# Head pairs in an attention, longer runs of expert weights, and expert pairs with few tokens laid out twice

## The chip, the cores and the metric

One core of one Trainium2 chip runs the whole program. The metric is the device time of one launch in microseconds (us).

The engines are named as the profile does: PE is TensorE's matmul, PEld its weight load, DVE is VectorE, ACT ScalarE, POOL GpSimd, SP SyncE, which here only issues DMAs. The kernel before took 2064.22 us, the median of three runs (2059.43 to 2067.44).

## The reference

A chain of two blocks on 256 tokens of width 1024, in float32. The first block has gated feed-forwards and two mixers; its first mixer (`combine_a`, `latent_attention`) is an attention of 8 query heads of width 64 over 512 keys (256 of the sequence, 256 of a context) beside a pooling branch. The second block has two layers; each has a mixer and then a mixture of experts:

```python
def grouped_moe(h, router_w, router_b, w_gate, w_up, w_down):
    t = h.reshape(B_ * S, D)
    scores = jax.nn.sigmoid((t @ router_w).astype(jnp.float32))
    ...
    top_w = top_s / jnp.sum(top_s, axis=-1, keepdims=True)
    combine = jnp.einsum('nk,nke->ne', top_w, jax.nn.one_hot(top_idx, N_EXPERTS, dtype=jnp.float32))
    for e in range(N_EXPERTS):
        he = jax.nn.silu(t @ w_gate[e]) * (t @ w_up[e])
        y = y + combine[:, e:e + 1] * (he @ w_down[e]).astype(jnp.float32)
```

There are 16 experts of width 512; each token goes to two of them. Gate and up are 1024 x 512, down is 512 x 1024, so an expert has 6 MB of weights in float32 and a layer 100.7 MB.

## The kernel before

**Layout.** The activations are held feature by token (`XT`, 128 x 8 x 256). Dense products in the earlier stages split both operands into a high and a low part and issue three products each (`mm3`, lines 448 to 450).

**Order of the work.** The kernel is written in Python on a framework that places the instructions of each engine in an order of its own, by priority and by when their inputs are there, and sets all semaphores; where `keep_in_program_order` or `pin` stands, the order of the text is kept. In the attention, `pipeline(units, width, bg, rate)` steps up to `width` units (Python generators) in turn, each from one `yield` to the next, and after each round takes `rate` steps of the background work `bg` (here dense products and the output projection).

**Attention of the first mixer** (`attend`, lines 1073 to 1107). A unit is one head for one block of 128 tokens: 16 units, 5 in flight. `t` is one of four pairs of heads, `tt` the token block, `s` which head of the pair; a head's features lie on partitions 0 to 63 or 64 to 127. A unit has four steps: the scores, one 128 x 512 product over 64 features (line 1079); the softmax on VectorE and ScalarE (lines 1082 to 1088); four transposes (line 864) and their copies; the product with the values (line 1100), four products that write 64 partitions of the tile `po`.

**The experts** (`moe`, from line 1578). Experts p and p + 8 make pair p; eight pairs run one after the other. A pair has 128 slots. The planner (lines 1739 to 1764, small VectorE operations after the router) counts the tokens of each expert and gives the two experts 64 and 64 slots, or 96 and 32 where one has over 64 tokens and the other at most 32; tokens that don't fit go to extra rounds at the end. `onehot` (line 1770) makes the 0/1 matrix that says which token sits in which slot; `gather` (line 1810) multiplies the normalised tokens `n_` by it and adds the modulation's shift `s`.

`pair` (line 1863) then runs gate and up (`products`, line 1841), each over eight blocks of 128 rows of K, for each block one product for each segment of slots. Its arms, chosen at run time by a register `gr_` that PE reads, are

```python
SEG = {2: ((0, 64, 0), (64, 64, 1)),
       3: ((0, 32, 0), (32, 32, 0), (64, 32, 0), (96, 32, 1)),
       1: ((0, 32, 0), (32, 32, 1), (64, 32, 1), (96, 32, 1))}
```

as (first slot, slots, expert). Each segment is a group of columns of the array with the slots as the stationary side and 512 weight columns moving; a float32 product is two instructions in the trace. After gate and up come SiLU (ScalarE) times up (VectorE), four transposes (line 1875) and a copy, the two halves of `down`, and `back`, which spreads the result over the tokens (line 1895). `nxt` places the next pair's gather between these steps.

**The weights of the experts.** `pieces` and `piece` issue them on SP's queue. A piece is 1 MB: half of K for gate and up, half of the columns for down, of one expert; 12 for a pair in the order gate, up, down, 96 for a layer. They go round a ring of 20 buffers; the DMA for piece n waits until PE has read piece n - 20. From piece 20 on, two pieces are loaded together in halves of 512 KB. Row k * 128 + p of the weights goes to partition p, so each partition gets 512 columns, 2 KB, from each of four rows.

Of the kernel before, what the change touches and what calls it, by code (L numbers as in the profile page):

```python
# [7 lines left out]
F32 = mybir.dt.float32  # L8
# [3 lines left out]
OP = mybir.AluOpType  # L12
# [5 lines left out]
KD = 8  # L18
# [107 lines left out]
def build(tc, I, out, dump=None, upto=99):  # L126
    nc = tc.nc
    coff, ctot = _const_layout()
    with ExitStack() as ctx:
# [831 lines left out]
        with ExitStack() as c1:  # L961
# [112 lines left out]
            def attend(t, tt, s):  # L1074

                hs = slice(s * 64, (s + 1) * 64)
                need(("A", t), "Ak", "Av")
                p = psum("sc")
                mm(p, qr[t][hs, tt * 128:(tt + 1) * 128], kr[hs, :], start=True, stop=True)
                yield  # L1080
                st = wk.tile([128, 4], F32, name="st", tag="st", bufs=8)
                V.reduce_max(st[:, 0:1], p, axis=AX.X)
                r = qs[:, t * 4 + tt * 2 + s:t * 4 + tt * 2 + s + 1]
                V.tensor_scalar(st[:, 1:2], st[:, 0:1], r, -1.0, op0=OP.mult, op1=OP.mult)
                x = tmp("e")
                S.activation(x, p, AF.Exp, bias=st[:, 1:2], scale=r, accum_out=st[:, 2:3])
                V.reciprocal(st[:, 3:4], st[:, 2:3])
                V.tensor_scalar(x, x, st[:, 3:4], None, op0=OP.mult)
                yield
                i0 = (t * 4 + tt * 2 + s) % 4 * 512  # L1090
                PT = pts[0][:, i0:i0 + 512].rearrange("p (a b) -> p a b", a=4)
                for _, pt in transposes([x[:, i * 128:(i + 1) * 128] for i in range(4)]):
                    V.tensor_copy(PT[:, 0:2], four(pt)[:, 0:2])
                    S.activation(PT[:, 2:4], four(pt)[:, 2:4], AF.Copy)
                yield
                if (tt, s) == (0, 0):
# [5 lines left out]
                if (tt, s) == (1, 1):  # L1102
# [34 lines left out]
            pipeline([attend(t, tt, s) for t in range(4) for tt in range(2) for s in range(2)], 5,  # L1137
                     [ch, part(op, 1), drain(), until(*[("Ao", t) for t in range(3)]), part(op, 2)], 0.8)
# [440 lines left out]
        def moe(l, a, op, pre=None, post=None):  # L1579


            with ExitStack() as c1:
# [3 lines left out]

                bufs = [hp.tile([128, KD * W], F32, name="ew", tag=t)[:, :2048] for t in ("hh", "hl")]
# [11 lines left out]
                def pieces(upto):  # L1599
                    while len(wpiece) < min(upto, len(todo)):  # L1600
# [3 lines left out]
                        for ks in (slice(0, 2), slice(2, 4)) if again else (slice(0, 4),):  # L1604
# [3 lines left out]
                def piece(buf, w, nm, hf, ks=slice(0, 4)):  # L1608
                    if nm == "exp_w_down_2":
                        w = w[:, hf * 512:(hf + 1) * 512]  # L1610
                    else:
                        w = w[hf * 512:(hf + 1) * 512]
                    w = w.rearrange("(k p) c -> p k c", p=128)
                    if isinstance(buf, list):
                        for k in range(ks.start, ks.stop):
                            nc.sync.dma_start(buf[k], w[:, k])
                    else:
                        nc.sync.dma_start(buf.rearrange("p (k c) -> p k c", k=4)[:, ks], w[:, ks])
# [5 lines left out]
                pieces(8)  # L1624

# [110 lines left out]

                A2 = [128, 2, 8]
# [10 lines left out]
                V.tensor_scalar(ga[:, 1], ga[:, 0], -1.0, 128.0, op0=OP.mult, op1=OP.add)  # L1748
                gi = mp.tile([128, 8], I32, name="gi")
                V.tensor_scalar(gi, ga[:, 0], 0.03125, None, op0=OP.mult)  # L1750
# [302 lines left out]
```

## Time and profile before

| | |
|---|---|
| time, three runs | 2064.22 us median (2059.43 to 2067.44) |
| the profiled execution | 2066.13 us, span 2064.4 us |
| PE busy | 1961.0 us, 95% of the span |
| VectorE, ScalarE busy | 1289.3 us (62%), 734.3 us (36%) |
| mean granted TensorE clock | 0.977 |
| DMA | 534.77 MB, 259 GB/s on average |
| attention of the first mixer | about 491 to 563 us |
| first expert stage, first gate product to last product | about 1413 to 1648 us |
| second expert stage | about 1819 to 2056 us |

A stage is found by its lines in the timeline of PE. "Busy" counts an engine's instructions from their start to a modelled end; products overlap, so the time that a product really takes is the distance of its start from the next one's. A wait is put down to what ended last before the instruction started; "issue" is time in which the engine waited for nothing that the profile shows. [...] A DMA's share can be above 1.00, as packets overlap.

### The profile page before, as it was taken

How to read it: one execution, taken by the hardware profiler on the slowest of the kernel's cores; microseconds unless marked ns; L12 is line 12 of the kernel's file. 1: busy time of each engine (PE TensorE's matmuls, PEld its weight loads, DVE VectorE, ACT ScalarE, POOL GpSimd, SP SyncE). 2: the span in 40 equal slices, each digit the busy share in tenths (PEclk: the TensorE clock that was granted, in tenths of full speed). 3: DMA queues.
4: the chain of work that ended last, by engine and by line, in shares of the span. 5: the costliest groups of instructions: out<-in, count | busy, mean ns of one | idle time of the engine just before them, and what ended most of it. 6: DMA issues, size and time to landing. Idle time of an engine off the chain costs nothing. (4 is left out here: it accounts for less than half of the span.)

```text
span 2064.4 us, 34691 instructions
## 1 busy us (share of the span) xinstructions
PE 1961.0 (95%) x14344; PEld 1605.7 (78%) x14344; DVE 1289.3 (62%) x2188; ACT 734.3 (36%) x1075; POOL 67.9 (3%) x60
## 2 busy tenths in 40 slices
PE   6999999999999999999999999997999799889998
PEld 5889899887699999999999999974444388744443
DVE  6357677758697979787797867853222387433222
ACT  3322222244354455445654445441000167500001
POOL 0000000011010010001010010000000010000000
PEclk8999999999999999999999999998999999889999
DMA  8678797734196959776496946479999654889995
GB/s 292 242 252 295 246 328 268 263 85 123 62 331 224 318 194 330 257 259 212 163 324 214 319 145 195 144 286 333 386 385 382 233 165 154 307 306 386 384 382 189
DMA packets 307696, 534.77 MB, mean 259 GB/s; under 512 B 12717, under 2 KB 167713, under 8 KB 294177
## 3 DMA queue, kind: packets, MB, share of 16 engines
q1 hardware_dynamic: 306960, 531.55, 73.5%
q8 instruction: 162, 2.65, 0.5%
q14 instruction: 46, 0.37, 0.1%
q10 hardware_dynamic: 528, 0.20, 0.0%
HBM read 530.64 MB, written 1.06 MB: 258 GB/s over the span
## 5 line engine op out<-in xcount | busy, mean ns | idle before, releaser
L448 PE MATMUL pa<-hh,whl 128*128 128x258 f32 (+1 forms) x880 | 252.3, 287 | 4.2 <-ACT hh L516 4.2
L449 PE MATMUL pa<-hl,whl 128*128 128x258 f32 (+1 forms) x880 | 249.3, 283 | 2.9 <-DVE hl L517 2.9
L448 PE MATMUL pb<-hh,whl 128*128 128x258 f32 (+1 forms) x880 | 249.1, 283 | 0.8 <-ACT s L564 0.8
L450 PE MATMUL pa<-hh,whl 128*128 128x258 f32 (+1 forms) x880 | 249.0, 283 | 0.0
L449 PE MATMUL pb<-hl,whl 128*128 128x258 f32 (+1 forms) x880 | 248.6, 282 | 0.0
L450 PE MATMUL pb<-hh,whl 128*128 128x258 f32 (+1 forms) x880 | 248.5, 282 | 0.0
L418 ACT ACTIVATE whl<-w13r 128x2048 fp32r<-128x2048 f32 x88 | 168.6, 1916 | 189.4 <-PE pb L450 93.6
L324 DVE SCALAR_TENSOR_TENSOR macc<-modw,cst,macc 128x1024 f32<-128x1024 f32 (+1 forms) x182 | 220.0, 1236 | 14.2 <-DMA modw<-in_w_mod_dram 13.5
L419 DVE TENSOR_TENSOR whl<-w13r,whl 128x2048 fp32r<-128x2048 f32 x88 | 201.7, 2292 | 39.8 <-ACT whl L418 39.8
L450 PE MATMUL py<-gh,whl 128*128 128x256 f32 (+1 forms) x704 | 216.8, 308 | 2.1 <-DVE whl L419 2.1
L448 PE MATMUL py<-gh,whl 128*128 128x256 f32 (+1 forms) x704 | 218.3, 310 | 0.1
L449 PE MATMUL py<-gl,whl 128*128 128x256 f32 (+1 forms) x704 | 216.3, 307 | 0.0
L448 PE MATMUL lin<-hh,whl 128*128 128x258 f32 x640 | 188.5, 295 | 5.7 <-DMA c_below<-in_consts_dram 5.0
L449 PE MATMUL lin<-hl,whl 128*128 128x258 f32 x640 | 182.2, 286 | 3.0 <-DVE hl L517 3.0
L450 PE MATMUL lin<-hh,whl 128*128 128x258 f32 x640 | 181.7, 284 | 0.0
L448 PEld LDWEIGHTS pa<-hh,whl 128*128 128x128 f32 x880 | 166.4, 189 | 12.2 <-ACT hh L516 4.4
L449 PEld LDWEIGHTS pa<-hl,whl 128*128 128x128 f32 x880 | 167.5, 190 | 3.5 <-DVE hl L517 3.3
L448 PEld LDWEIGHTS pb<-hh,whl 128*128 128x128 f32 x880 | 166.6, 189 | 1.8 <-ACT s L564 1.0
L450 PEld LDWEIGHTS pa<-hh,whl 128*128 128x128 f32 x880 | 167.1, 190 | 0.4 <-issue 0.4
L450 PEld LDWEIGHTS pb<-hh,whl 128*128 128x128 f32 x880 | 166.5, 189 | 0.4 <-issue 0.4
L449 PEld LDWEIGHTS pb<-hl,whl 128*128 128x128 f32 x880 | 166.7, 189 | 0.0
L418 ACT ACTIVATE whl<-w2r 128x768 fp32r<-128x768 f32 (+3 forms) x80 | 90.7, 1143 | 161.0 <-PE py L450 95.7
(444 smaller groups left out, 3796.6 us busy)
## 6 DMA issues: line engine op xcount, KB each, us to landing
w13r<-in_ffn_w_dram SPq DMA_DIRECT2D x86, 1024.0 KB
modw<-in_w_mod_dram SPq DMA_DIRECT2D x62, 1024.0 KB
ew<-in_exp_w_down_dram SPq DMA_DIRECT2D x108, 512.0 KB
modw<-in_ada_w_dram SPq DMA_DIRECT2D x48, 1024.0 KB
ew<-in_exp_w_gate_dram SPq DMA_DIRECT2D x92, 512.0 KB
ew<-in_exp_w_up_dram SPq DMA_DIRECT2D x92, 512.0 KB
w2r<-in_ffn_w_dram SPq DMA_DIRECT2D x18, 1536.0 KB
ew<-in_exp_w_gate_dram SPq DMA_DIRECT2D x16, 1024.0 KB
```

What stands on the lines that cost most here:

```text
L324: V.scalar_tensor_tensor(acc[h], x, c, acc[h], op0=OP.mult, op1=OP.add)
L418: S.activation(h, src, AF.Copy)
L419: V.tensor_sub(l, src, h.bitcast(F32))
L448: mm(p, ah, bh, start=start, stop=False)
L449: mm(p, ah, bl, start=False, stop=False)
L450: mm(p, al, bh, start=False, stop=stop)
```

## The change

**Attention.** A unit is now a pair of heads: `attend(t, tt)`, 8 units, 3 in flight, 1.1 background steps for each round in place of 0.8. The two score products stand next to each other, and the value products of the two heads alternate.

```diff
-                p = psum("sc")
-                mm(p, qr[t][hs, tt * 128:(tt + 1) * 128], kr[hs, :], start=True, stop=True)
+                ps, xs, pt_ = [psum("sc") for _ in range(2)], [], []
+                for s, p in enumerate(ps):
+                    hs = slice(s * 64, (s + 1) * 64)
+                    mm(p, qr[t][hs, tt * 128:(tt + 1) * 128], kr[hs, :], start=True, stop=True)
...
                 for i in range(4):
-                    mm(po[hs, tt * 128:(tt + 1) * 128], vn[:, i, s * 64:(s + 1) * 64], PT[:, i], start=i == 0,
-                       stop=i == 3, skip_group_check=True)
+                    for s in range(2):
+                        mm(po[s * 64:(s + 1) * 64, tt * 128:(tt + 1) * 128], vn[:, i, s * 64:(s + 1) * 64], pt_[s][:, i],
+                           start=i == 0, stop=i == 3, skip_group_check=True)
...
-            pipeline([attend(t, tt, s) for t in range(4) for tt in range(2) for s in range(2)], 5,
-                     [ch, part(op, 1), drain(), until(*[("Ao", t) for t in range(3)]), part(op, 2)], 0.8)
+            pipeline([attend(t, tt) for t in range(4) for tt in range(2)], 3,
+                     [ch, part(op, 1), drain(), until(*[("Ao", t) for t in range(3)]), part(op, 2)], 1.1)
```

**Runs of 8 KB.** Partition p now gets neighbouring rows of the weights: for gate and up rows 8p to 8p + 7, in two pieces of four rows; for down rows 4p to 4p + 3, in two pieces of two full rows. A piece is one run of 8 KB for each partition. A piece of down now holds half of K and all columns. Pieces are loaded in halves only from piece 84 on.

```diff
-                        for ks in (slice(0, 2), slice(2, 4)) if again else (slice(0, 4),):
+                        for ks in (slice(0, 2), slice(2, 4)) if n >= 84 else (slice(0, 4),):
...
-                    if nm == "exp_w_down_2":
-                        w = w[:, hf * 512:(hf + 1) * 512]
-                    else:
-                        w = w[hf * 512:(hf + 1) * 512]
-                    w = w.rearrange("(k p) c -> p k c", p=128)
+                    w = w.rearrange("(p h k) c -> h p (k c)", p=128, h=2)[hf]
...
-                        nc.sync.dma_start(buf.rearrange("p (k c) -> p k c", k=4)[:, ks], w[:, ks])
+                        cs = slice(ks.start * 512, ks.stop * 512)
+                        nc.sync.dma_start(buf[:, cs], w[:, cs])
...
-                            products(pd, hT, 4, lambda k: (w_("exp_w_down_2", dd), k), gr_, ks)
+                            products(pd, hT, 4, lambda k: (w_("exp_w_down_2", k // 2), k % 2 * 2 + dd), gr_, ks)
```

The features have to be permuted to match: the normalised tokens are written so when they leave PSUM, and the shift `s` takes the same order by a DMA to DRAM and one back, on ScalarE's queue.

```diff
+                by_p = dr.tile([8, 128], F32, name=f"by_p{l}")
+                nc.scalar.dma_start(by_p.rearrange("k p -> p k"), s)
+                sP = mp.tile([128, KD], F32, name="sP")
+                nc.scalar.dma_start(sP, by_p.rearrange("a b -> (a b)").rearrange("(p k) -> p k", k=KD))
...
-                        S.activation(n_[:, tt, i * 512:(i + 1) * 512], pT[tt, i], AF.Copy, scale=rst[:, tt:tt + 1])
+                        S.activation(n_[:, tt].rearrange("t (k p) -> t k p", k=KD)[:, :, i * 64:(i + 1) * 64],
+                                     pT[tt, i].rearrange("t (p k) -> t k p", k=KD), AF.Copy, scale=rst[:, tt:tt + 1])
```

**Light pairs.** Where both experts of a pair have at most 32 tokens, the planner gives them slots 0 to 31 and 32 to 63, and `onehot` sets the same tokens again in slots 64 to 127. A fourth arm runs four column groups: the first copy over the first half of K, the second over the other half.

```diff
+                light = mp.tile([128, 8], F32, name="light")
+                V.tensor_mul(light, c32[:, 0], c32[:, 1])
+                l64 = mp.tile([128, 8], F32, name="l64")
+                V.tensor_scalar(l64, light, 64.0, None, op0=OP.mult)
...
+                V.tensor_add(gf[:, 0], l64, ga[:, 0])
+                V.tensor_scalar(gi, gf[:, 0], 0.03125, None, op0=OP.mult)
+
+                V.scalar_tensor_tensor(gf[:, 1], light, -32.0, ga[:, 0], op0=OP.mult, op1=OP.add)
...
+                    def arm_light():
+                        h = n_k // 2
+                        for k in range(h) if ks is None else range(ks[0] // 2, ks[-1] // 2 + 1):
+                            for o in range(4):
+                                ws, kp = w_(k + o // 2 * h)
+                                mm(p[o * 32:o * 32 + 32, :], x[:, k + o // 2 * h, o * 32:o * 32 + 32], ws[o % 2][kp],
+                                   start=k == 0, stop=k == h - 1, skip_group_check=True)
...
                         with tc.If(gr_ == 2) as c:
                             arm(2)
                         with c.Else():
-                            with tc.If(gr_ == 3) as c2:
-                                arm(3)
-                            with c2.Else():
-                                arm(1)
+                            with tc.If(gr_ == 4) as c1_:
+                                arm_light()
+                            with c1_.Else():
+                                with tc.If(gr_ == 3) as c2:
+                                    arm(3)
+                                with c2.Else():
+                                    arm(1)
```

The copies are added when gate and up are turned: in every pair, each of the two results is copied out of PSUM, and four products with a 128 x 128 matrix take the place of the four transposes. `summing` makes that matrix with one VectorE operation: the identity, with a second diagonal 64 apart in a light pair. SiLU and the multiplication follow on the turned results. The stationary side of these products is read with a step of four floats.

```diff
+                    def turned(raw):
+                        p = psum("tr")
+                        for i in range(4):
+                            pin(mm(p[:, i * 128:(i + 1) * 128], raw.rearrange("s (j k) -> s k j", k=4)[:, i], sm_,
+                                   start=True, stop=True))
+                        return p
                     products(pg, xg_b, KD, lambda k: (w_("exp_w_gate_2", k // 4), k % 4), gr_)
+                    graw, uraw = tm(), tm()
+                    S.activation(graw, pg, AF.Copy)
                     products(pu, xg_b, KD, lambda k: (w_("exp_w_up_2", k // 4), k % 4), gr_)
-                    act = tm()
-                    S.activation(act, pg, AF.Silu)
-                    V.tensor_mul(act, act, pu)
+                    tg = turned(graw)
+                    V.tensor_copy(uraw, pu)
                     sw, ohT = pl
+                    hT_ = tm()
+                    S.activation(hT_, tg, AF.Silu)
                     nxt(0)
-                    hT = four(tm())
-                    p = psum("tr")
-                    for i in range(4):
-                        pin(PE.transpose(p[:, i * 128:(i + 1) * 128], act[:, i * 128:(i + 1) * 128], ident))
-                    V.tensor_copy(hT, four(p))
+                    tu = turned(uraw)
+                    V.tensor_mul(hT_, hT_, tu)
+                    hT = four(hT_)
                     nxt(1)
```

## Rows read from the trace of the kernel before

**Rows 1.** Windows, core 0, three stretches; columns: us, busy (x instructions) per engine, clock, DMA, GB/s

```profile
491.00:563.00 72.00, 68.11 (x386) 45.89 (x385) 49.97 (x132) 30.60 (x71) 0.00 (x0) 0.95 0.15 46
1413.00:1648.00 235.00, 223.26 (x1195) 105.61 (x1194) 63.41 (x134) 18.57 (x28) 0.00 (x0) 0.99 0.96 351
1819.00:2056.00 237.00, 225.98 (x1588) 104.67 (x1587) 62.14 (x132) 16.76 (x26) 0.00 (x0) 0.99 0.93 341
```

**Rows 2.** Waits of PE, 1412:1648; columns: us in total, times, longest us

```profile
PE ga L1817 <- issue: 5.9, 3, 2.3
PE pu L1848 <- issue: 2.0, 1, 2.0
```

**Rows 3.** Waits of PE, 1818:2064

```profile
PE pu L1848 <- issue: 2.6, 1, 2.6
PE pu L1848 <- DMA ew<-in_exp_w_down_dram: 2.1, 1, 2.1
```

**Rows 4.** Timeline of SP's DMA issues, 1735:2050; columns: start us, us, engine line op

```profile
1802.11 4.66 SPq L1616 DMA_DIRECT2D ew<-in_exp_w_up_dram  x4
1823.68 5.48 SPq L1618 DMA_DIRECT2D ew<-in_exp_w_down_dram  x8
```

**Rows 5.** Timeline of PE, pair 4 of the second expert stage, 1937:1966

```profile
1937.43 7.09 PE L1848 MATMUL pg<-ew,nx 128*64 128x512 f32 x32
1944.35 7.04 PE L1848 MATMUL pu<-ew,nx 128*64 128x512 f32 x32
1951.32 2.05 PE L1817 MATMUL ga<-oh,nx 128*128 128x128 f32 x16
1953.21 0.60 PE L1875 MATMUL tr<-c_ident,tm 128*128 128x128 f32 x4
1953.64 1.95 PE L1817 MATMUL ga<-oh,nx 128*128 128x128 f32 x16
1955.52 7.09 PE L1848 MATMUL pd<-ew,tm 128*64 128x512 f32 x32
1962.54 1.22 PE L1895 MATMUL py<-dd 128*128 128x256 f32 x8
...
1965.30 7.09 PE L1848 MATMUL pg<-ew,nx 128*64 128x512 f32 x32
```

**Rows 6.** DMA view, 1820:2040; columns: queue, packets, MB, share of 16 engines

```profile
q1 hardware_dynamic: 41440, 79.70, 98.5%
q8 instruction: 32, 0.52, 1.0%
```

**Rows 7.** Timeline of PE, pair 1 of the second expert stage, 1848:1863

```profile
1848.19 7.07 PE L1848 MATMUL pg<-ew,nx 128*32 128x512 f32 x64 [0.95 <-PE py L1895]
1855.09 7.05 PE L1848 MATMUL pu<-ew,nx 128*32 128x512 f32 x64
```

**Rows 8.** DMA view, 1841:2036

```profile
DMA packets 38442, 74.34 MB, mean 381 GB/s; under 512 B 2353, under 2 KB 2353, under 8 KB 38411
```

**Rows 9.** DMA view, 566:570

```profile
DMA packets 224, 1.70 MB, mean 426 GB/s; under 512 B 16, under 2 KB 16, under 8 KB 16
```

**Rows 10.** Timeline of VectorE, 1809:1813

```profile
1811.87 0.42 DVE L1773 TENSOR_TENSOR oh<-c_iota,slot 128x256 f32<-128x256 f32 x1
```

**Rows 11.** Timeline of PE, attention of the first mixer, 488:566

```profile
491.63 1.13 PE L1079 MATMUL sc<-kr,qr 64*128 64x512 f32 x4
...
497.24 1.12 PE L1079 MATMUL sc<-kr,qr 64*128 64x512 f32 x2
...
501.36 1.09 PE L1100 MATMUL po<-pts,vn 128*64 128x128 f32 x8
```

**Rows 12.** Windows, core 0, two stretches of the same attention

```profile
510.00:520.00 10.00, 9.19 (x55) 6.26 (x54) 9.49 (x27) 5.49 (x13) 0.00 (x0) 1.00 0.39 124
520.00:530.00 10.00, 8.23 (x30) 4.82 (x30) 6.18 (x16) 3.84 (x10) 0.00 (x0) 0.66 0.27 86
```

**Rows 13.** Page, part 5: the costliest groups

```profile
L448 PEld LDWEIGHTS pa<-hh,whl 128*128 128x128 f32 x880 | 166.4, 189 | 12.2 <-ACT hh L516 4.4
```

More of the change, by code (lines that the diff above doesn't have):

```diff
@@ L1080, in attend @@
                 yield
[L1081 to L1088, printed above, removed]
@@ L1089, in attend @@
-                yield
[L1090 to L1094, printed above, removed]
+                for s, p in enumerate(ps):
+                    st = wk.tile([128, 4], F32, name="st", tag="st", bufs=8)
+                    V.reduce_max(st[:, 0:1], p, axis=AX.X)
+                    r = qs[:, t * 4 + tt * 2 + s:t * 4 + tt * 2 + s + 1]
+                    V.tensor_scalar(st[:, 1:2], st[:, 0:1], r, -1.0, op0=OP.mult, op1=OP.mult)
+                    x = tmp("e")
+                    S.activation(x, p, AF.Exp, bias=st[:, 1:2], scale=r, accum_out=st[:, 2:3])
+                    V.reciprocal(st[:, 3:4], st[:, 2:3])
+                    V.tensor_scalar(x, x, st[:, 3:4], None, op0=OP.mult)
+                    xs.append(x)
@@ L1095, in attend @@
+                yield
+                for s, x in enumerate(xs):
+                    i0 = (tt * 2 + s) * 512
+                    PT = pts[0][:, i0:i0 + 512].rearrange("p (a b) -> p a b", a=4)
+                    for _, pt in transposes([x[:, i * 128:(i + 1) * 128] for i in range(4)]):
+                        V.tensor_copy(PT[:, 0:2], four(pt)[:, 0:2])
+                        S.activation(PT[:, 2:4], four(pt)[:, 2:4], AF.Copy)
+                    pt_.append(PT)
                 yield
-                if (tt, s) == (0, 0):
+                if tt == 0:
@@ L1772, in onehot @@
                     oh = mp.tile([128, 2, 128], F32, name="oh", tag="oh")
-                    V.tensor_tensor(oh, iota1[:, None, :].to_broadcast([128, 2, 128]),
-                                    slot[:, :, p:p + 1].to_broadcast([128, 2, 128]), op=OP.is_equal)
+                    V.tensor_tensor(oh[:, :, 0:64], iota1[:, None, 0:64].to_broadcast([128, 2, 64]),
+                                    slot[:, :, p:p + 1].to_broadcast([128, 2, 64]), op=OP.is_equal)
+                    V.scalar_tensor_tensor(oh[:, :, 64:128], iota1[:, None, 64:128].to_broadcast([128, 2, 64]),
+                                           l64[:, p:p + 1], slot[:, :, p:p + 1].to_broadcast([128, 2, 64]),
+                                           op0=OP.subtract, op1=OP.is_equal)
                     return oh
@@ new lines, in summing, with pair @@
+                def summing(p):
+                    x = (w0, w1)[p % 2]
+                    i2 = ident.rearrange("p (h j) -> p h j", h=2)
+                    V.scalar_tensor_tensor(x.rearrange("p (h j) -> p h j", h=2), i2[:, ::-1, :], light[:, p:p + 1], i2,
+                                           op0=OP.mult, op1=OP.add)
+                    return x
+                def pair(pl, w_, gr_, sm_, nxt=lambda i: None, last_=False):
+                    pg, pu = psum("pg"), psum("pu")
+                    def turned(raw):
[4 more added lines that the diff above has]
+                        return p
@@ L1919, in reg @@
                 def reg(p):
-                    return nc.values_load(gi[0:1, p:p + 1], engines=[ENG.PE], min_val=1, max_val=3)
+                    return nc.values_load(gi[0:1, p:p + 1], engines=[ENG.PE], min_val=1, max_val=4)
                 regs = {0: reg(0)}
@@ L1941, in moe @@
                         ohs[p + 1] = onehot(p + 1)
-                    pair(pl[p], lambda nm, hf: [wpiece[p, e, nm, hf] for e in range(2)], regs[p], nxt, p == 7)
+                    pair(pl[p], lambda nm, hf: [wpiece[p, e, nm, hf] for e in range(2)], regs[p], summing(p), nxt, p == 7)
                     pieces(12 * p + 12 + RING)
@@ L2000, in w_ @@
                         return got[nm, hf]
-                    pair(places(oh2, w2_, 0), w_, None, last_=True)
+                    pair(places(oh2, w2_, 0), w_, None, ident, last_=True)
         op = even(mods["a0"])
```

14 lines of the change are left out of this document (6 added, 8 removed).

## The prediction

> **What bounds the kernel now.** I read the page first, then the stretches, the waits and the timeline of the three stages that the change touches, then the DMA view.
>
> The page calls PE 95% busy over the whole span, which says little by itself, because stages with different limits are averaged. By stretch [rows 1], PE is busy 68.1 of 72 us in the attention of the first mixer, 223.3 of 235 in the first expert stage and 226.0 of 237 in the second. DMA runs at 0.15, 0.96 and 0.93 of its capacity there. So in both expert stages two resources look full at once, and the waits have to say which one PE is held by. In the first expert stage PE's two largest waits are "issue", 5.9 and 2.0 us, in which it waits for no data, and no wait on weights is listed [rows 2]. In the second there is one wait on weights, 2.1 us [rows 3]. PE is therefore the bound of both, with DMA just behind it. The reason DMA can hide at all is the ring of 20 weight pieces, which is full when a stage begins: the last pieces are issued at 1802.11, the next ones at 1823.68, when the first pair has used some up [rows 4].
>
> One expert pair on PE is read off the start times [rows 5]: gate 6.92 us, up 6.97, gather 1.89, transposes 0.43, gather 1.88, down 7.02, the rest 2.76 to the next gate; 27.87 in all, 223 for eight. The 76 pieces that are not in the ring at the start are 79.7 MB, which is what the SP queue moved from 1820 to 2040 [rows 6].
>
> **The expert pairs, part by part.** The trace doesn't show how many tokens an expert has. The reference's routing, worked out on its inputs, gives for the eight pairs of the first layer 52/29, 24/50, 16/20, 50/55, 9/48, 29/33, 26/18, 32/21, and of the second 12/79, 12/81, 28/72, 22/78, 21/17, 25/8, 20/14, 14/9. The four pairs with 72 to 81 tokens are those that run in 32-slot segments (x64 in place of x32) [rows 5, 7], so trace and counts agree. Both counts at most 32: pairs 2, 6 and 7 of the first layer, 4 to 7 of the second; seven light pairs.
>
> *Every pair* loses its four transposes (0.43) and gets two sets of four 128x128 float products. Eight such products are one gather, 1.88 [rows 5], so a set is 0.94 and the pair 27.87 - 0.43 + 1.88 = 29.32; sixteen pairs cost 16 x 1.45 = 23.2 us more. The two copies out of PSUM lie beside PE: the gate's copy runs under the up product, the up's copy under the first set, SiLU under the gather, the multiplication under the second gather. In each layer's last pair there is no gather, so its multiplication is bare, but so were the old multiplication and copy; that is 0.
>
> *A light pair* runs gate, up and down with four column groups at a time, over half of K. That four 32-column groups run at full rate is shown: 64 instructions of 32 columns start 6.90 us before the next product, and 32 of 64 columns take 6.92 [rows 5, 7]. Half as many steps halve 6.92 + 6.97 + 7.02, a saving of 10.45 us. Seven pairs: 73.2.
>
> *Its code* is the open cost. Each product carries one arm more (80 matmuls become 96), and a light pair takes its instructions away faster. From 1820 to 2040, 32 instruction packets of 16 KB arrive, some four per pair [rows 6]; 20% more products make it nearly five, in 19 us in place of 28. The stalls called "issue" are 1.97 us each (5.9 in three) [rows 2]. Nothing per light pair is the one end; a stall of 2 us for each of five blocks, 10 us, the other. I take 3 us, one and a half such stalls, since today one pair in two has a stall with four blocks. Seven pairs: 21. [...]
>
> *8 KB runs.* With 2 KB runs the saturated stretch moves 381 GB/s [rows 8]; a stretch with almost nothing but 8 KB packets moves 426 [rows 9]. That one lasts 4 us, so I take 415 and keep 381 and 426 as ends. By itself this is worth nothing, since PE doesn't wait for weights. It decides whether the faster PE is fed: 79.7 MB take 192 us at 415 and 209 at 381. About 11 us of the 218 before were gaps while the ring waited for slots; I keep them. The last piece is then there some 205 us after the first gate, and 10 us of work follow it.
>
> *Sum by stage.* First layer: 5 x 29.32 + 3 x (18.87 + 3) = 212.2 in place of 223.0, so 235 becomes 224; its last weights are wanted at 214, there at 205. Second layer: 4 x 29.32 + 4 x 21.87 = 204.8, so 237 becomes 219; wanted at 209, there at 205. At the old rate they would be there at about 219 to 222, and 9 us of the second layer's gain and 5 of the first's would go. Fewer, larger DMAs cost SP less issuing; the splitting in halves now begins at piece 84, so a freed half is refilled up to 3.5 us later, which the 4 us of slack take. All four down pieces are now wanted before the first half of down: 3.5 us earlier, inside the 10.
>
> *Small work.* The planner gains four tiny VectorE operations and one more one-hot operation on the path to the first gather, where PE waits; the one-hot took 0.42 [rows 10] and is split in two. At about 0.1 us each that is 0.5 per layer, 1 in all. The block that adds the two copies is one VectorE operation per pair, and VectorE is busy 63 of 235 us [rows 1]. The two DMAs on ScalarE's queue (shifts to DRAM and back) need only the modulation, long known, and are wanted 40 us later at the first gather. If ScalarE had to wait for the round trip it would hold up the weight halves of the output projection; I put that at 0, and up to 5 us per layer into the range.
>
> **The head pairs.** Two score products that happen to stand next to each other, on rows 0 to 63 and 64 to 127, take 1.13 us together, and a single one 1.12 [rows 11]. Fifteen stretches become eight: 7 x 1.06 = 7.4 us of PE. The value products are eight instructions in 1.02 us for one head [rows 11], and two heads write different column groups; up to 8 x 1.02 = 8.2. So 15.6 us of PE at most. But VectorE is busy 9.5 of 10 us at 510 to 520, and the clock already fell to a mean of 0.66 at 520 to 530 behind a gap [rows 12]; VectorE's 50 us of 72 [rows 1] would be 50 of 56. Ends 0 and 15.6; I take half, 8, and name VectorE's softmax chain as what is late next.
>
> **Sum.** -10.8 - 18.2 + 1 - 8 = -36. The profiled execution took 2066.1 us (span 2064.4), 1.9 above the median of the runs shown, so 2030, or 1.7% less.
>
> **The rivals.**
> *The strided loads (slower).* The new products read their stationary side with a step of four floats; no row shows such a load. Sixteen loads per pair, 256 in all. They decide from 36 / 256 = 0.14 us each on. If each adds the 0.19 of a whole ordinary load [rows 13], 49 us go: 2079. For it: PE is the bound of both stages. Against it: loads run beside products, and the gather's are hidden today. [...] Chance 0.08.
> *Code instead of arithmetic.* Light pairs run at the pace of their instruction blocks: with 7 us lost per light pair in place of 3, 2058; with all 10.45 lost, 2082. For it: "issue" is already PE's largest wait. Against it: pairs in 32-column segments issue twice the instructions and wait no more [rows 3]. Chance 0.13.
> *8 KB runs no faster.* 14 us go: 2044. Against it are the 426 [rows 9]. Chance 0.08.
> *It doesn't take the light arm*, because counts differ: 23 + 1 - 8 = 16 us more, 2082. Chance 0.02.
> *VectorE holds the attention*: nothing of the 8, 2038; inside the main case.
>
> **How the numbers follow.** The main case has 0.69. Its ends: no code loss gives 21 us, of which the second layer, then bound by DMA, keeps only 4 of 12, so 13; attention gives 8 more: 2009, and the best rate 5 more. Upwards: attention 8, the round trip up to 10, code 3 more per light pair, 21, but not all of it together. I say 2004 to 2058. A measurement of this kernel tells about 0.5% (10 us) from no change: faster means below 2054. The main case, the DMA rival and a small part of the code rival lie there: 0.81. Near no change: half of the code rival and the mild strided loads, 0.10. Slower: 0.09.
>
> **What would show it.** In the profile after: light pairs with gate, up and down at 3.4 to 3.5 us, the two sets at 0.94 each; weights at 410 or more with 8 KB packets; the expert stages near 224 and 219 us; score products x4 eight times at 1.13. It is wrong if the sets take 1.5 us or more, if PE's "issue" waits grow by more than 6 us per light pair, or if a new wait on weights stands first among PE's waits in the first layer.

## The result, and the profile after

The changed kernel takes 2112.5 us (median of four runs, 2109.0 to 2115.9), the kernel before 2065.4 in the same comparison: a ratio of 1.023 (1.0215 to 1.0248), slower by 47 us where 35 us less had been forecast. Its profiled execution has a span of 2109.2 us, against 2064.4.

Lines of the page of the changed kernel: span, clock and DMA by slices, and the two queues that matter here, that of the instructions (q8) and that of the shift's DMAs (q10).

```profile
span 2109.2 us, 34931 instructions
...
PEclk8999999999999999999999999989899899899998
DMA  8678687643687598857588563579999236698992
...
q8 instruction: 176, 2.88, 0.6%
q10 hardware_dynamic: 2896, 0.21, 0.1%
```

The clock dips in five of the last 14 slices, where it dipped in three before. 176 packets of 16 KB are loaded by the instruction queue; they were 162. Such a packet is called a block here. Now the expert stages, as windows from the first gate to the end of the last down product, which leaves out the tail that the windows of [rows 1] take in; first the kernel before, then the changed one (columns as in [rows 1]).

```profile
1413.00:1645.00 232.00, 221.78 (x1187) 104.53 (x1186) 60.95 (x130) 15.57 (x25) 0.00 (x0) 0.99 0.97 355
1819.00:2052.00 233.00, 223.81 (x1576) 103.15 (x1576) 60.65 (x129) 15.10 (x23) 0.00 (x0) 0.99 0.94 345
```

```profile
1410.00:1665.00 255.00, 227.47 (x1289) 124.54 (x1287) 64.50 (x143) 21.50 (x34) 0.00 (x0) 0.94 0.83 324
1838.00:2096.00 258.00, 218.45 (x1672) 118.22 (x1673) 63.39 (x140) 21.15 (x32) 0.00 (x0) 0.94 0.79 312
```

Read to the tenth off the first and last product, 231.5 us became 253.9 in the first stage and 232.3 became 257.4 in the second: 47.5 us in both, about the whole loss. PE's busy time hardly moved (221.8 to 227.5, 223.8 to 218.5), though seven pairs have half the products: part of the busy time is now at a lower mean clock (0.94, it was 0.99), the turned sets came on top, and the rest of the growth is idle time. The DMA share fell from 0.97 and 0.94 to 0.83 and 0.79: for the most part the weights wait for PE, not PE for them. PE's waits say for what; first stage, then second (us in total, times, longest):

```profile
PE tr L1915 <- issue: 11.8, 5, 5.0
PE pu L1882 <- DMA ew<-in_exp_w_up_dram: 5.0, 2, 3.0
PE ga L1843 <- issue: 3.4, 2, 1.8
PE py L1949 <- ACT dd L1941: 2.2, 2, 1.4
PE pu L1874 <- DMA ew<-in_exp_w_up_dram: 2.2, 1, 2.2
```

```profile
PE pu L1882 <- issue: 13.2, 4, 6.6
PE pu L1874 <- issue: 9.5, 3, 4.3
PE tr L1915 <- issue: 4.2, 2, 2.6
PE ga L1843 <- issue: 4.0, 1, 4.0
PE py L1949 <- issue: 2.6, 2, 2.3
PE pu L1882 <- DMA ew<-in_exp_w_up_dram: 2.5, 1, 2.5
```

All "issue" waits of the two stages add up to 53 us; they were 12, of which [rows 2, 3] show the larger ones. Waits on weights are 9.7 us; they were 2.1. What the "issue" waits wait for can be read from the packet records: 19 of them are longer than 1 us, 49 us in all, and each of the 19 ends 1.2 to 2.0 us after a block has been loaded. It was so before (six waits, 1.3 to 2.3 us after a block). So these are waits for code. One light pair of the second stage (pair 6), PE's timeline, then windows of it:

```profile
2046.82 3.64 PE L1882 MATMUL pg<-ew,nx 128*32 128x512 f32 x32
2057.08 5.50 PE L1882 MATMUL pu<-ew,nx 128*32 128x512 f32 x32 [6.62 <-issue]
2062.57 2.13 PE L1915 MATMUL tr<-w,tm 128*128 128x128 f32 x8
2064.54 1.95 PE L1843 MATMUL ga<-oh,nx 128*128 128x128 f32 x16
2066.33 2.03 PE L1915 MATMUL tr<-w,tm 128*128 128x128 f32 x8
2068.19 1.95 PE L1843 MATMUL ga<-oh,nx 128*128 128x128 f32 x16
```

```profile
2050.00:2057.00 7.00, 0.46 (x8) 0.00 (x0) 0.00 (x0) 0.60 (x1) 0.00 (x0) 0.79 1.03 414
2057.00:2063.00 6.00, 5.92 (x34) 1.82 (x34) 0.34 (x1) 0.00 (x0) 0.00 (x0) 0.68 1.02 405
2063.00:2071.00 8.00, 8.00 (x60) 7.28 (x63) 2.43 (x4) 0.60 (x1) 0.00 (x0) 1.00 0.23 90
```

Three things are seen in the timeline. The gate is as short as forecast (3.64 listed, half of the 7.09 in [rows 5]). Then PE stands for 6.62 us with nothing that it waits for but its instructions (a block is loaded from 2054.25 to 2055.27, and PE goes on at 2057.08), and the up product behind that takes 5.50 in place of 3.64. (The second of the windows has the granted clock of that product, the number before the last two: a mean of 0.68; in windows of 1 us it is 0.50 from 2057 to 2060, 0.56 in the next and 1.00 from 2061 on.) And a turned set, the four products that turn gate or up, holds the next work off for 1.97 us (2062.57 to 2064.54), the other for 1.86, where 0.94 had been forecast.

From gate to gate the changed kernel's pairs take 31.1, 33.2, **33.6**, 34.1, 34.4, 35.2, **31.7**, **20.5** us in the first layer and 31.4, 35.1, 38.7, 37.3, **31.4**, **34.8**, **29.6**, **19.0** in the second (light pairs bold; the last of a layer to the end of its down product). Without a stall an ordinary pair would take 31.1 to 31.4 with these sets, a light one 10.45 less, about 20.8. So the light pairs lose all that they save, the last of each layer aside, and seven of the nine ordinary pairs lose 2 to 7.5 us too.

### The profile page after: what moved, and what is told of

Same layout as the page of the kernel before. It is cut to its first block, busy times and chain, and to the rows that moved or that the text cites. A ratio compares the mean times of both kernels' runs of the same rounds, so it can differ in the third digit from the quotient of the medians.

```text
span 2109.2 us, 34931 instructions
## 1 busy us (share of the span) xinstructions
PE 1949.0 (92%) x14536; PEld 1636.3 (78%) x14536; DVE 1295.3 (61%) x2228; ACT 743.0 (35%) x1091; POOL 64.6 (3%) x60
## 5 line engine op out<-in xcount | busy, mean ns | idle before, releaser
L448 PEld LDWEIGHTS pa<-hh,whl 128*128 128x128 f32 x880 | 166.7, 189 | 11.8 <-ACT hh L516 4.0
```

The source lines that it names most:

```text
L448: mm(p, ah, bh, start=start, stop=False)
```

## The experiments

**Four kernels on the code and the loads.** unit_step moves the step of four out of TensorE's loads:

```diff
-    S.activation(graw, pg, AF.Copy)
+    S.activation(four(graw), pg.rearrange("s (j k) -> s k j", k=4), AF.Copy)
-    V.tensor_copy(uraw, pu)
+    V.tensor_copy(four(uraw), pu.rearrange("s (j k) -> s k j", k=4))
-    mm(p[...], raw.rearrange("s (j k) -> s k j", k=4)[:, i], sm_, ...)
+    mm(p[...], raw[:, i * 128:(i + 1) * 128], sm_, ...)
```

> The changed kernel, with the step of four moved out of TensorE's loads: the two copies out of PSUM write the halves in turned order, and the eight new loads of a pair read whole runs. Theory (two causes): the strided loads cost 0.12 us each (a set starts its next work after 1.97 and 1.86 us where a gather of twice as many instructions takes 1.95), and the rest of the loss is code: the 16 KB instruction blocks of the expert stages come about 6 us apart, whatever part of them runs. Then the sets fall to about 0.95 us, the five ordinary pairs of the first layer get shorter by 1.9 us each, and the pairs that wait for code (the light ones, and the second layer's) gain little: 2090 to 2104 us in all. Rival (the loads are the whole loss): sixteen pairs gain 1.9 us each, 31 us, 2081 or less.

Measured: 2087.2 us, 1.0107 (1.0080 to 1.0134) of before; 25 us less than the changed kernel. PE's timeline of unit_step, first layer's first pair:

```profile
1426.36 1.16 PE L1915 MATMUL tr<-w,tm 128*128 128x128 f32 x8
1427.36 1.95 PE L1843 MATMUL ga<-oh,nx 128*128 128x128 f32 x16
1429.14 1.06 PE L1915 MATMUL tr<-w,tm 128*128 128x128 f32 x8
1430.04 1.95 PE L1843 MATMUL ga<-oh,nx 128*128 128x128 f32 x16
```

The sets take 1.00 and 0.90 us: what was forecast, once the step is gone. The groups of PEld show the loads themselves, first of the changed kernel, then of unit_step (x count, busy us, mean ns):

```profile
L1915 PEld LDWEIGHTS tr<-w,tm 128*128 128x128 f32 x256 | 62.1, 327 | 32.3 <-issue 32.3
```

```profile
L1915 PEld LDWEIGHTS tr<-w,tm 128*128 128x128 f32 x256 | 32.8, 201 | 32.1 <-issue 32.1
```

A strided load lasts 327 ns on the mean, a plain one 201. The step costs 1.93 us per pair, 31 us of PE in sixteen. It shows as 25, between the two texts (2090 and more, 2081 or less) and in neither: the stalls took back a part of it. What is left over before, 23 us, is something else.

no_light and no_arm3 are unit_step with one arm less each (the choice of arms in short; no_light also calls no pair light); light_first asks for the light arm first.

```diff
 with tc.If(gr_ == 2): arm(2)
-elif (gr_ == 4): arm_light()      # no_light
-elif (gr_ == 3): arm(3)           # no_arm3
 else: arm(1)
```

> As unit_step, without the fourth arm: no pair is light, each product has the three arms of the kernel before; the turned sums, the 8 KB runs and the head pairs stay. Code theory: the light arm saves nothing, since a light pair takes as long as its code, and its code slows the others; without it every pair goes at TensorE's pace, 29.3 us, the issue waits of the expert stages fall from 53 us to about those of the kernel before (12), and the time is 2065 - 2 + 23 = 2086, at or below unit_step. Rival (the arm does save its arithmetic, and what was lost is elsewhere): 7 x 10 us slower than unit_step, 2150 or more.

Measured: 2072.6, 1.0027 (1.0008 to 1.0045). Issue waits of the stages 11.8 us, about as in the kernel before, and pairs of 29.2 us where none stalls. Taking the light arm away makes the kernel 15 us *faster*: there it saved nothing. The time is 13 below the 2086 expected, and the trace puts that into the expert stages: together they are 11 us longer than in the kernel before (474.8 for 463.9), where the turned sets were to cost 23. An ordinary pair without a stall costs 1.3 us more, not 1.45, and the stalls beside it some 9 us less in all. The first gate comes 2.7 us earlier, about as the text had it.

> As unit_step, without the arm for 96 slots of the first expert and 32 of the second, which no pair of these inputs takes (a general kernel needs it). Nothing that runs is changed; 32 + 32 + 32 instructions' worth of loads and products (a third of the products' code) is gone from every pair. Code theory (blocks come one after another, taken or not): a pair has 1.5 blocks less, 9 us, so the light pairs fall from 30 to 34 us to 20 to 24, the issue waits mostly go, and the time is 2025 to 2050. Rival (what stalls is the taken jump, each by a fixed 2 to 5 us, however much code lies between): the light pairs jump as before, only the four pairs in the last arm jump less far; within 10 us of unit_step.

Measured: 2023.7, 0.9798 (0.9781 to 0.9815), 63 us less than unit_step, a little more than expected. In this kernel the arm for 96/32 slots is left out, which no pair of these inputs takes; all that runs is the same. The page's line of the instruction queue, the windows of its stages, and PE's timeline of one light pair (the fifth of the second layer):

```profile
q8 instruction: 152, 2.49, 0.5%
```

```profile
1412.00:1623.00 211.00, 201.97 (x1290) 102.72 (x1289) 64.45 (x143) 21.47 (x34) 0.00 (x0) 1.00 0.96 390
1797.00:2009.00 212.00, 200.95 (x1679) 98.10 (x1678) 64.19 (x142) 21.29 (x33) 0.00 (x0) 0.99 0.93 378
```

```profile
1914.41 3.64 PE L1882 MATMUL pg<-ew,nx 128*32 128x512 f32 x32
1917.87 3.62 PE L1882 MATMUL pu<-ew,nx 128*32 128x512 f32 x32
1921.42 1.16 PE L1912 MATMUL tr<-w,tm 128*128 128x128 f32 x8
```

24 blocks fewer than the 176, 1.5 per pair, for an arm that never ran: its code, though jumped over, was fetched all the same. The light pairs fall to 19.0 to 23.2 us (the last of the second layer takes 29.3, since there weights become late: 6.9 us of waits on them in that stage), the clock is back at 1.00 and 0.99, the weights move at 390 and 378 GB/s, and the issue waits are 8.5 us. The rival, a fixed price per taken jump, wanted no change here. A price that grows with the length of the jump is not ruled out by this kernel alone, since the light arm's jump is shorter in it too.

> As unit_step, with the arms in another order: the light arm is asked for first, then 64/64, then the two others. The same code, the same work. Code theory: the sum of blocks is the same, so within 8 us of unit_step. Rival (taken jumps): a light pair falls into its arm without a jump, and an ordinary one jumps; the seven light pairs lose their stall before each product (2 to 5 us each, three of them per pair), at least 20 us faster in the second layer, and the five ordinary pairs of the first layer get slower.

Measured: 2075.0, 1.0051 (1.0033 to 1.0068), 12 us less than unit_step. Neither text fits. In the profiles, 7.7 us apart, the first stage is 5.1 us shorter, but the second, where the jumps should have told most, is 0.9 longer, and 3 us come off between the stages, where nothing was changed. The seven light pairs still take 28.5, 31.4, 16.7 and 30.2, 32.5, 26.9, 17.0 us. So the rival's theory of the jumps is not borne out, and why the kernel is 12 us faster stays open.

**Why a block takes so long.** thin_weights is unit_step with a quarter of the bytes of every piece after the first twenty of a layer, so most of the expert weights are left out:

```diff
+if len(wpiece) >= RING:
+    ks = slice(ks.start, ks.start + 1)
 cs = slice(ks.start * 512, ks.stop * 512)
```

> unit_step, with a quarter of the bytes for every weight piece after the first twenty of a layer (the rest of such a buffer keeps what it held: most of the expert weights are left out). Code, branches and products are the same. Theory (a block takes 6 us because it shares the transfer engines with the weights): the blocks come 3.3 to 4 us apart as they do behind the last weights of the changed kernel, 5.3 of them take 17 to 21 us, and the light pairs fall to TensorE's 19 to 21 us: 2015 to 2035. Rival (6 us is what a block takes whatever else moves): the gaps stay at 5.9, the light pairs at 29 to 35 us, and only the weight waits (7 us) go: 2078 to 2088.

Measured: 2021.6, 0.9796 (0.9777 to 0.9816). The gaps between the starts of the 16 KB blocks in the two expert stages, from the traces' packet records (a quarter of the gaps are shorter than the lower quarter):

```
kernel         blocks   median gap us   lower quarter us
before             69            6.32               5.97
after              82            5.97               5.56
unit_step          82            5.84               5.64
no_arm3            58            6.80               5.93
thin_weights       82            4.37               3.57
```

With full weight traffic the lower quarter is at 5.6 to 6.0 us, before and after alike; with a quarter of the traffic it is 3.6. The changed kernel shows the same within one trace: its 38 gaps with over 380 GB/s of traffic are 5.5 us or longer, and of the 15 with under 100 GB/s the lower quarter is 3.3. In thin_weights the issue waits fall from 53 us to 18 with the code as it was, and the light pairs to 21.6 to 24.7 (not quite the 19 to 21 expected), the last of a layer to 17. So what a block takes depends on the weights that move beside it. The block's own packet lasts about 1 us in unit_step and thin_weights alike (median 1.05 and 0.96); what grows is the time between two of them, and where it is spent no record shows.

At the pace of the lower quarter the blocks of unit_step alone take 462 us (82 x 5.64), and its two stages last 479. Those of no_arm3 take 344 (58 x 5.93), and its stages last 421.

**The parts alone, on the kernel before.** heads_only has the head pairs and nothing else, runs8_only the 8 KB runs (with the activation's product written in turned order, so that the transposes read whole runs).

> The kernel before with the head pairs of the first mixer alone. The first gate of the changed kernel starts 2.4 us earlier than in the kernel before, so this part is worth about 2 to 3 us: 2062, ratio 0.998 to 1.0. As predicted before the change ran it would be 8 us (2057); if it is over 5 us, something between the mixer and the experts gave back the rest.

Measured: 2049.2, 0.9928 (0.9911 to 0.9944): 15 us, not 2. The first gate starts 7.2 us earlier (1405.8 for 1413.0), and the two expert stages are 3.5 and 3.7 us shorter, from first gate to last down product, without any change to them. The expectation was wrong since it read the part off the changed kernel, where something else had taken a part of the gain back; the next paragraphs show what. The score products stand as forecast: in the changed kernel seven of the eight pairs take one stretch like this (PE's timeline), and the two products of the eighth stand apart, at 1.12 each:

```profile
493.59 1.13 PE L1081 MATMUL sc<-kr,qr 64*128 64x512 f32 x4
```

> The kernel before with the 8 KB runs of expert weights alone (the activation's product is written in turned order, so the four transposes read whole runs). Theory: the blocks of instructions come some 6 us apart with 2 KB and with 8 KB packets alike (5.93 in both traces), TensorE doesn't wait for weights, so nothing changes: 2060 to 2068, with weights at 410 GB/s in full stretches. Rival (longer packets hold up the instruction blocks, and the issue waits of 4 to 6.6 us in the changed kernel, where they were 2 to 2.6, come from that): the issue waits of the expert stages grow from 12 to 25 us or more, and the time to 2080 or more.

Measured: 2067.1, 1.0014 (1.0005 to 1.0024). The issue waits are 4.7 us, so longer packets do not hold up the instructions, and that rival is gone. But its first gate comes at 1419.7, 6.8 us late. The way there: a wait of PE on VectorE (pa on whl) of 4.0 to 5.1 us, at 765 to 778 us, that stands in all eight profiles with the change's 8 KB layout and its way of turning the shift (4.6 here, 4.2 in the changed kernel), and in neither before nor heads_only. VectorE's timeline of the changed kernel:

```profile
753.81 0.47 DVE L659 SCALAR_TENSOR_TENSOR XT<-py,hg_f,XT 128x256 f32<-128x256 f32 x1
761.45 1.41 DVE L322 TENSOR_SCALAR macc<-modw,cst 128x1024 f32<-128x1024 f32 x2 [7.17 <-DMA modw<-in_ada_w_dram]
762.78 2.28 DVE L419 TENSOR_TENSOR whl<-w13r,whl 128x2048 fp32r<-128x2048 f32 x1
```

VectorE is held by a weight of the modulation, 7.17 us. The transfer that was in its way is the shift's, issued by ScalarE at 743.60: 1040 packets of 4 bytes, all between 747.6 and 749.7 us. changed_shift is the changed kernel, strided loads and all, with these packets replaced (the addresses cut short):

```diff
-nc.scalar.dma_start(by_p.rearrange("k p -> p k"), s)
-nc.scalar.dma_start(sP, by_p....)
+PE.transpose(pS[0:KD, 128:256], s, ident)
+V.tensor_copy(w1[0:KD, :], pS[0:KD, 128:256])
+nc.gpsimd.dma_start(by_p, w1[0:KD, :])
+nc.gpsimd.dma_start(sP, by_p....)
```

> The changed kernel (strided loads and all four arms kept) with another way for the shifts: one TensorE transpose on the way to the first router sum, a copy, eight rows of 512 bytes to DRAM and back, on GpSimd's queue, in place of 1024 elements of 4 bytes on ScalarE's. Theory: in every run with the 8 KB layout these 4-byte packets (1040 of them at 746 to 750 us) fall among the modulation weights, the rate drops from 396 to 16 GB/s there, VectorE waits 7.2 us for a weight and TensorE 4 to 5 us for VectorE, in the feed-forward that follows; without them that wait goes and the first gate starts 5 to 7 us earlier: 2104 to 2108, against 2112.5 of the changed kernel. Rival (the wait comes from the placement of other work after the shorter attention): the wait stays and the time with it.

Measured: 2099.3, 1.0175 (1.0154 to 1.0197), 13 us less than the changed kernel by the medians (12 by the ratios to before), and below its range. The windows around the spot, of the changed kernel and of changed_shift (the last column is GB/s):

```profile
746.00:749.00 3.00, 3.00 (x27) 3.00 (x27) 1.89 (x3) 1.98 (x3) 0.32 (x2) 1.00 1.60 343
749.00:754.00 5.00, 5.00 (x45) 5.00 (x44) 4.22 (x6) 1.98 (x3) 2.34 (x2) 1.00 0.82 78
```

```profile
746.00:749.00 3.00, 3.00 (x28) 3.00 (x27) 2.57 (x5) 1.98 (x3) 1.00 (x2) 1.00 1.06 364
749.00:754.00 5.00, 5.00 (x45) 5.00 (x45) 3.89 (x5) 1.98 (x3) 2.31 (x2) 1.00 1.08 382
```

For five us the weights go at 78 GB/s in place of 382, while 4 KB are moved; by the packet records, 8 KB packets of weights that start in this stretch last up to 4.7 us; without the small packets their median is 0.31. Without these the wait of PE is gone and the first gate starts at 1404.1, 6.5 us earlier than in the changed kernel. Another 6.9 us of the profile lie in the first expert stage (247.0 for 253.9), whose code is the same, and 2 us are lost again behind it. The new way differs in size of packet, queue and moment at once (its DMAs are issued at 1365 and 1371 us), so the run doesn't tell these apart. The second layer's 1040 packets, at 1139 to 1151 us, slow the weights too (90 GB/s at 1142 to 1148, for 332 in changed_shift), but PE waits for no more than 0.7 us there.

**Does the place of the code in its blocks matter?** heads_only and changed_shift both gained in stages that they did not touch, so before_pad puts 39 more small transposes, 78 instructions, ahead of all later code of the kernel before. At 64 bytes each, an estimate from no_arm3 (24 blocks of 16 KB for that arm's 384 loads and products in each of 16 pairs), that is 5 KB:

```diff
-PE.transpose(p[:, :n], r[:n, :], ident[:n, :n])
+for _ in range(40 if name == "a" else 1):
+    PE.transpose(p[:, :n], r[:n, :], ident[:n, :n])
```

> The kernel before, with one small transpose at its start done forty times over, so that all later code of TensorE stands 5 KB further on in its 16 KB blocks; nothing else. Theory (of the 15 us that the head pairs alone were worth, 7 come before the first gate and the others from stalls for code that fell elsewhere): where blocks end moves the stalls of the expert stages, and the time moves by 3 to 8 us one way or the other, beside some 4 us for the transposes themselves. Rival (the placement of code does nothing): 2064 to 2069 with the same issue waits, 5.9 and 2.0 us in the first expert stage.

Measured: 2063.9, 1.0003 (0.9991 to 1.0014): no change. The stalls do move (in the first stage from the first, fourth, seventh and eighth pair to the third and sixth, and its length from 231.5 to 227.5 us), but the second stage keeps its length (232.2 for 232.3). So the part of those gains that lies in untouched stages is not explained: 7 us of heads_only and 7 of changed_shift stay open. Stage lengths are from one execution each, and the executions of the kernel before alone spread over 10 us (2057.5 to 2067.4), so a stage's 3 or 4 us may be no more than that.

**Put together.** swap keeps all cases covered with less code. From the third pair of a layer on, the heavier expert of a 96/32 pair comes first, by the source address of its weights and by its slots, so that one arm serves for both kinds. It also asks for the light arm first, as light_first does (in short):

```diff
-piece(buf, I[nm][l, p + 8 * e], nm, hf, ks)
+piece(buf, I[nm][l][bass.ds(spr[p, e], 1)]..., nm, hf, ks)      # p >= 2
+gf[:, 0] += 2 * sw32; gf[:, 1] -= sw32; slots of the first expert += 3 * sw32
 light arm, else arm(2), else:
-    arm(3) if gr_ == 3 else arm(1)
+    arm(3)                                                       # p >= 2
```

> unit_step with less code: from the third pair of a layer on, the expert with the more tokens of a 96/32 pair is put first, by a register in the source address of its weights and by its slots, so that one of the two arms with 32-slot segments does for both; the light arm is asked for first. All cases stay covered. 12 of 16 pairs lose a third of the products' code, 1.5 blocks. Code theory: most of the gain of no_arm3 (63 us against unit_step, of which 12 pairs in 16 lose the arm): 2027 to 2045. Rival (the addresses from a register hold SyncE up, so weights come late): waits on weights stand first, 2060 or more.

Measured: 2031.0, 0.9845 (0.9828 to 0.9863), with 158 blocks; waits on weights 6.1 us. Of the 56 us against unit_step, 12 may belong to the order of the arms and not to their length. swap_shift adds the shift's new way:

> swap with the shifts taken over in that way: all that was found, put together. Theory: the 5 to 7 us of the shift's packets come off the 2031 of swap: 2023 to 2027. Rival: no difference from swap.

Measured: 2023.6, 0.9811 (0.9795 to 0.9828), 7 us less than swap. That beats both kernels, by 39 and by 89 us, and it lies where the prediction had put the change (2030). swap_no_light is the same without its light arm:

> swap_shift without the light arm: no pair is light, the turned sums stay. It tells what half of the work is worth once the code lets it through. Theory: in swap_shift a light pair takes 16 to 24 us, an ordinary one 29.2, so the seven light pairs cost 29.2 again (25 the last of a layer): 29.2 x 14 + 25 x 2 = 459 us for both stages, in place of 427, with fewer stalls for code, so 2050 to 2058. Rival (code was all; the arm does nothing even now): 2018 to 2026, since less code is fetched.

Measured: 2059.9, 0.9986 (0.9974 to 0.9998), just above its range; pairs of 29.2 us, issue waits 5.5. So the light arm is worth 36 us as soon as the code lets it through, and it cost 15 where it didn't.

## Why the prediction was wrong

**The step that failed is the price of the code**, "I take 3 us, one and a half such stalls, since today one pair in two has a stall with four blocks". It was worked out from the stalls that the waits list [rows 2], as if a stall were an event with a fixed price. The blocks are a chain with a pace of its own. [rows 6] had it: 32 blocks in 220 us, one every 6.9 us, four in a pair of 27.9, while the packet records of that trace put the lower quarter of the gaps at 6.0. So a pair needed 24 to 26 us for its code (69 blocks in the two stages, 4.3 per pair) where it needed 27.9 for its arithmetic; there was hardly any room. The change adds an arm to every product: 82 blocks, 5.1 per pair, 29 to 31 us. That is about the time the light pairs took, 29.6 to 34.8 (last ones aside), though their arithmetic needs 20.8: they lose 8.8 to 14.0 us each where 3 had been put. And the ordinary pairs lose too, for which the text put nothing: the nine lose 30 us together over 31.2 each, 17 of them listed as issue waits and 2 as a wait on weights. The rival "code instead of arithmetic" (0.13) was the right one, but its worst case, all 10.45 us lost in each light pair, gave 2082 since it too priced only the light pairs.

The argument against that rival, that pairs in 32-column segments issue twice the instructions and wait no more [rows 3], does not bear on it. What was fetched did not depend on what was issued: no_arm3 fetches 24 blocks less for an arm that never ran. Whether a taken jump waits by itself, no run here tells from the wait for the chain.

**The turned sets, 0.94 us each**: 1.97 and 1.86. The term of +1.45 per pair was +3.4. It counted the instructions rightly (1.00 and 0.90 without the step) and left the step at nothing. That was the strided loads' rival (0.08): it asked for 0.14 us per load to decide, and 0.12 was measured, 31 us of the 36. The loads took 327 ns on the mean with the step of four floats, 201 without; why, no run shows. The step's 31 us alone would have made the forecast 2061, no change; with the code it made a loss. It is also the one of the prediction's signs of being wrong that showed plainly (a set of 1.5 us or more).

**The shift's two DMAs, put at 0**: ScalarE did not hold PE up, as the text had it, but the weights of the modulation came late. 1024 elements of 4 bytes held them up for some 5 us, some 660 us ahead of the gather that wanted the shift, because the DMA was issued as soon as its modulation was known. Replacing them gave 12 to 13 us in the changed kernel, 6.5 of them before the first gate, and 7 in swap. The bound of 5 us per layer was too tight for the first, and the mechanism named was not the one.

**The 8 KB runs** were right: nothing alone (1.0014 with the shift's cost in it), and a full stretch of 10 us in the changed kernel, 1850 to 1860, runs at 426 GB/s, near the 415 taken. Fewer, larger DMAs did cost SP less issuing: 97 issues of expert weights took 49 and 43 us in the two stages, where 158 had taken 82 and 91. The rate is needed only by the faster PE: 390 and 378 GB/s in no_arm3. There the second layer's last pair does wait for weights, so the margin that the text saw there ("wanted at 209, there at 205") is none.

**The head pairs**: 8 us forecast, ends 0 and 15.6; 15 measured alone. By the start of the feed-forward behind the mixer 5.4 us are won (574.9 for 580.3), by the first gate 7.2, near the 8; the rest lies in stages whose code is untouched, without a cause that was shown. With the same attention the feed-forward of the changed kernel starts 14.5 us earlier (565.8), that of its variants 8 to 11; why it varies so stays open. Of the 14.5 us, 12 were lost before the first gate, the 4.2 us wait behind the shift among them.

**The light pairs' arithmetic** was right: 3.46 and 3.55 us from one product's start to the next where nothing stalled (the light pair shown of no_arm3), and light pairs of 19.0 to 23.2 us in no_arm3 (but for the last of the second layer) against 18.9 + 3. The chance of 0.81 for "faster" rested on a mean price where a floor was at work.

## What to carry to other kernels

Where arms are unrolled in code, work out a pace for the code as for an engine: blocks per stage by the gap between their packets where they come closest. If that pace is near the stage's own, cutting arithmetic may give nothing and an added arm may make even the work outside it slower, as here: unit_step's blocks alone take 462 of the 479 us of its stages, and it is 15 us faster without the light arm. Cut code first, arms that never run too (63 us in no_arm3). And look at what a small transfer of single elements runs beside at the moment it is issued (the shift's took the rate of the others from 382 to 78 GB/s for 5 us); here that was when its input was ready, not where its result was needed.

## What the runs showed of the hardware that was not expected

- Instruction blocks of 16 KB came 5.6 to 6.0 us apart (lower quarter of the gaps) under 310 to 390 GB/s of weights, with packets of 2 KB and of 8 KB alike, and 3.6 us apart under 117 to 121 GB/s (thin_weights), though the block's own packet lasted 1 us in both. An arm that was never taken was fetched (24 blocks for 16 pairs, no_arm3).
- A 128x128 float load from every fourth element took 327 ns on the mean and held the next instruction back by 0.12 us (the changed kernel); a plain one, 201 ns (unit_step).
- Beside 1040 packets of 4 bytes (4 KB) the other transfers of 5 us went at 78 GB/s, 382 without them; in a second place at 90 over 6 us, for 332.
- A stall cost more than its wait where the clock fell. Behind the wait of 6.62 us the clock of the up product was 0.68 on the mean, and it took 5.50 us in place of 3.64; over the two stages the granted clock was 0.94, and 0.99 to 1.00 in no_arm3, where the issue waits were 8.5 us and not 53.
